# Side work spread inside the dense units: the delta rule's steps in a one-core hybrid flow step

## The chip, the core and the metric

The kernel runs on one core of a Trainium2 chip. The core has a matrix engine (TensorE, here PE, whose weight loads are listed apart as PEld), a vector engine (VectorE, DVE), a scalar engine (ScalarE, ACT), GpSimd (POOL) and SyncE (SP), which here issues most of the transfers (DMA). Each engine works off its own list of instructions, and semaphores order the lists against each other. The metric is the device time of one execution in microseconds (us); less is better.

## What is computed

The reference is one layer of a hybrid backbone, for 2048 tokens of one group (`x_sample`) and 128 of another (`x_prompt`), with D_MODEL = 1024 and branches of width 512. One wide projection feeds three token mixers, whose gated outputs are projected back and merged:

```python
proj = jnp.einsum('btd,de->bte', xn, w_in)
qkv, beta, dec, z_a, u_b, v_b, z_b, x_c, z_c, gates = jnp.split(proj, points, axis=-1)
qkv = short_conv(qkv, conv_w)
...
o, s_f, s_b = delta_bidir(q, k, v, g, beta, s0_f, s0_b)      # branch A: gated delta rule
o_a = (rmsnorm(o, o_norm_g) * jax.nn.silu(z_a)).reshape(B, T, W_BR)
o_b = chunk_sgu(u_b, v_b, sgu_norm_g, w_spatial, b_spatial) * jax.nn.silu(z_b)   # branch B
o_c = fourier_mix(x_c, grid) * jax.nn.silu(z_c)                                  # branch C
pb = jnp.einsum('btnw,nwd->btnd', br, w_branch)
merged = jnp.einsum('btnd,btnd->btd', jax.nn.sigmoid(gates), pb)
return jnp.einsum('btd,de->bte', merged, w_out), s_f, s_b
```

The delta rule goes over the tokens in chunks, forwards and backwards. Within a chunk a triangular system is solved, and from chunk to chunk a 128x128 state per head (four heads) is carried:

```python
def step(s, inp):
    u0_, w_, qk_, qg_, kd_, gl_ = inp
    u = u0_ - jnp.einsum('bhck,bhkv->bhcv', w_, s)
    o = jnp.einsum('bhck,bhkv->bhcv', qg_, s) + jnp.einsum('bhij,bhjv->bhiv', qk_, u)
    s = gl_[..., None, None] * s + jnp.einsum('bhck,bhcv->bhkv', kd_, u)
    return s, o
```

## The kernel before

**Dense work.** The normalised tokens lie in SBUF as two float16 halves, `xh` and `xl`. Every weight block of 128 columns is loaded by SP into one of two staging tiles `wst` (`read_w`, L185), squared and summed on ACT (L194), turned into a power-of-two scale (`scales`, L165 to L178: a cast and four small integer operations on DVE, L170 to L177, and one tiny matmul `wscb`), and split by ACT (L200) and DVE (L201) into the halves `whi` and `wlo`. A product is then three float16 matmuls for each 128 rows of the contraction. `gemm_T` makes outputs with channels on the partitions, for token blocks of 512 (the last has 128: `TBS`). `gemm_N` makes outputs with tokens on the partitions, 128 columns at a time in the V and Fourier stages, 512 at a time in the output stage. A dense *unit* is one such output block of eight 128-row products. All PE work goes through the helper `mm` (L159 and L160), so dense matmuls and many side matmuls carry L160; transposes have the lines of their callers.

**Stages, in order of the span.** Modulation and the first normalisation with the gate of branch A (to about 150 us); twelve q/k/v units with their convolution (to about 430); V of branch B with its spatial matmul (`wsT`, to about 560); U and the gate of branch B (from about 566 to 775); the Fourier branch (four channel groups, from about 775 to 1100: x columns by `gemm_N`, row transforms through the tiles `X20`, `X21`, then the gate); the branch projections and merges; the output projection.

**Side work.** The delta rule has little work per step and long chains of dependence, so its instructions are emitted in between. `delta()` is a Python generator that yields after each step: for each of 17 chunks `prep` (norms of q and k, transposes, the products k·k and q·k, stores), for each block of four chunks `base_inverse` (the inverse of 32x32 triangles on DVE: the tiles `XB` and `E`, loaded from DRAM by L713, started by the copy L716 after eight empty steps, then 31 rounds of L723 and L724), and then two scans of 17 chunks (`scan_dir`, `level`, `attend`). An earlier generator, `decays()`, makes the decay factors during the q/k/v stage.

**Pace.** The class `Pace` holds one generator. After a unit the kernel calls `pace.tick(us)` with the unit's length in us; the length is added up, and for every `quota` (1.2 us in `decays()`, 1.6 in `delta()`) one step is taken. A unit of 512 tokens counts 5.12 us, so three or four steps are emitted one behind another after it. `tick` also calls `weight_step()`, which takes one step of the weight pipeline: a load, or one of the three parts of a conversion.

**Who decides the order.** Python's order of emission is a priority. A scheduler orders each engine's list by these priorities and by its own model of when operands are ready; evictions of dense results stand under `tc.high_priority()`. The list that results is fixed, and on the chip each engine keeps to it. The PSUM banks of dense units come from a pool of three (`ps_mm`), those of side work from `ps_d`, and `ps_x` holds two more.

Of the kernel before, what the change touches and what calls it, by code (L numbers as in the profile page):

```python
# [20 lines left out]
P = 128  # L21
# [89 lines left out]
def hybrid_flow_kernel(ctx: ExitStack, tc: tile.TileContext, x_prompt, x_sample, state_delta, c, c_ctx, ln_g, w_ada,  # L111
# [44 lines left out]
    mhalf = sb(cp, [P, 1], "mhalf")  # L156
    G.memset(mhalf, -0.5)

    def mm(out, l, r, start=True, stop=True):  # L159
        PE.matmul(out, l, r, start=start, stop=stop)  # L160

    def rsqrt(out, ss, mul, w):
        G.tensor_scalar(out, ss, mul, EPS, ALU.mult, ALU.add)
# [60 lines left out]
    w_in_, w_ada_, b_ada_ = w_in[0], w_ada[0], b_ada[0]  # L224
    xs_, xp_ = x_sample[0], x_prompt[0]
# [84 lines left out]
    PE.transpose(pp.rearrange("p g k -> p (g k)"), prc, ident[:16, :16])  # L310
    sc = sb(cp, [P, 2, KT], "sc")
    A.activation(sc, pp, AF.Sigmoid)
    scT = sb(cp, [P, KT, 2], "scT")
# [5 lines left out]
    def columns():  # L319
        SY.dma_start(prm[0:8, :], ln_g.rearrange("o (k p) -> (o k) p", p=P))  # L320
        SY.dma_start(prm[8:44, :], conv_w[0].rearrange("t (k p) -> (t k) p", p=P))
        SY.dma_start(prm[44:48, :], sgu_norm_g.rearrange("o (k p) -> (o k) p", p=P))
        SY.dma_start(prm[48:49, :], o_norm_g)
        SY.dma_start(prm[49:65, :], b_ada[0, 0:2 * D].rearrange("(k p) -> k p", p=P))
        pp = bank(ps_x, [P, NPRM])
        PE.transpose(pp, prm, ident[:NPRM, :NPRM])
        V.tensor_copy(pc, pp)

    convw = lambda j, ct: pc[:, 8 + j * 12 + ct:8 + j * 12 + ct + 1]
# [26 lines left out]
    for blk in range(8):  # L356
        if blk == XB:
            load_x(*TBS[0])
            columns()
        ps = bank(ps_d, [2, 256])  # L360
        for k0 in range(0, KT, 4):
            st = sb(p0p, [P, 4, 256], "ast", bufs=8)
            last_ada = SY.dma_start(st, w_ada_[k0 * P:(k0 + 4) * P, blk * 256:(blk + 1) * 256].rearrange("(k p) c -> p k c", p=P))
            if k0 and blk in AD:
                acc = sb(p0p, [P, 2, 256], "aacc")
                ada_sum(acc, st, range(k0, k0 + 4))
                for g in range(2):
                    mm(ps, sel[:, g, :], acc[:, g, :], False, g == 1)
                continue
            for k in range(4):  # L370
                mm(ps, scT[:, k0 + k, :], st[:, k, :], k0 + k == 0, k0 + k == KT - 1)
        adr = sb(p0p, [2, 256], "adr")
        V.tensor_copy(adr, ps)
        for k in range(2):
            PE.transpose(pa[:, blk * 2 + k, :], adr[:, k * P:(k + 1) * P], ident[:2, :2])
    ms = sb(cp, [P, KT, 2], "ms")
    sh = sb(cp, [P, KT, 2], "sh")
    with tc.high_priority():
# [23 lines left out]
    for ti, (t0, tn) in enumerate(TBS):  # L402
# [13 lines left out]
        for k in range(KT):  # L416
            ps = bank(ps_d, [P, tn])
            for j in range(nt):
                PE.transpose(ps[:, j * P:(j + 1) * P], xt[:, j, k * P:(k + 1) * P], ident)
# [30 lines left out]
    def decays():  # L450
# [60 lines left out]
        gamR = dram("gamR", [2, NCH * H, P])  # L511
        for d in range(2):
            pt = bank(ps_d, [HN, P])
            PE.transpose(pt, flat(gam)[:, d * HN:(d + 1) * HN], ident)
# [111 lines left out]
    def prep(g, ci, t, nxt, held):  # L626
# [5 lines left out]
        def turned(part):  # L632
            ps = bank(ps_d, [P, WB])
            for h in range(H):
                PE.transpose(ps[:, hs(h)], cur[part][:, h, :], ident)  # L635
            return ps

        def norm(ps, i):
# [22 lines left out]
        T = sb(d2, [P, WB], "T")  # L661
        ps = bank(ps_d, [P, WB])
        for h in range(H):
            PE.transpose(ps[:, hs(h)], tok[:, 0, hs(h)], ident)
        A.copy(T, ps)
        A.dma_start(kTD[t], T)
        more(2, lambda: rows(2, nxt))
# [244 lines left out]
    def finish(t, o):  # L912
# [7 lines left out]
        V.tensor_tensor(h3(o), h3(o), bc(ss, P), ALU.mult)  # L920
        ps = bank(ps_out, [P, WB])
        for h in range(H):
            PE.transpose(ps[:, hs(h)], o[:, hs(h)], ident)  # L923
# [72 lines left out]
    vw = getw(4, 1)  # L996
    ps = bank(ps_x, [P, 4, P])
    for g in range(4):
        PE.transpose(ps[:, g, :], wsn[:, g, :], ident)
    V.tensor_copy(wsT, ps)  # L1000
    vinv = sb(ep, [P, 4], "vinv", bufs=1)
    for i in range(4):
# [383 lines left out]
```

## Time and profile before

| | |
|---|---|
| time, median of 3 runs | 2290.28 us (2284.63 to 2294.26) |
| time of the profiled execution | 2289.02 us |
| its span, first to last instruction | 2287.2 us |
| mean granted clock of PE | 0.993 |
| busy, share of the span | PE 97%, DVE 56%, ACT 34%, POOL 38% |
| matmul groups at L160 with 128x512 outputs, `xh·whi`, `xh·wlo`, `xl·whi` | 2080 each, 702.3, 703.9 and 704.3 us busy |
| ACT's wait for `wst` ahead of L194, in all | 174.2 us, 47 times, longest 10.7 |

A row of the timeline reads: start and duration in us, engine, line, operation, written tile <- read tiles, operands, the number of instructions merged into the row, and in brackets the idle time of the engine just before it with what ended it. A matmul's duration contains its way through the array: 128x512 matmuls that last 0.38 us each start 0.216 us apart. A float32 matmul is recorded as two passes. A row of the busy time by stages reads: stretch and its length, then busy time and number of instructions of PE, PEld, DVE, ACT and POOL, the granted clock of PE, the share of DMA, and GB/s. A row of the waits reads: total us, how often, the longest.

### The profile page before, as it was taken

The numbers are of one execution on the slowest core, as the hardware profiler recorded it, in microseconds if no ns is written. First come the engines' busy times: TensorE is split into PE (matmuls) and PEld (weight loads), VectorE is DVE, ScalarE is ACT, GpSimd is POOL, SyncE is SP. The second block draws the span as 40 slices with busy tenths as digits, with TensorE's granted clock in tenths as the row PEclk, the third lists the DMA queues.
The fourth block names the chain that finished last, engine by engine and source line by source line (L and its number), as shares of the span: only waits on it lengthen the run. The fifth ranks groups of instructions, "written<-read, shape, count | busy, mean of one in ns | idle before, by whom it ended". The sixth has DMA issues, their size and how long they took to land.

```text
span 2287.2 us, 43200 instructions
## 1 busy us (share of the span) xinstructions
PE 2229.7 (97%) x17076; PEld 1365.7 (60%) x17076; DVE 1283.9 (56%) x3001; ACT 769.0 (34%) x1485; POOL 861.3 (38%) x1090
## 2 busy tenths in 40 slices
PE   7999999999999999999999999999999999999998
PEld 3564444798555787788566666566665444444443
DVE  5637744496857666455655446756665443333454
ACT  3544633322333332332422223433322332222232
POOL 1421332253546430553433324355653121122643
PEclk9999999999999999999999999999999999999999
DMA  8416722376777543343634344655554444332542
GB/s 275 144 52 205 245 103 81 115 226 162 232 216 227 161 139 69 117 134 108 206 122 133 122 133 140 205 161 171 171 158 149 148 131 130 111 114 95 186 150 101
DMA packets 320628, 345.92 MB, mean 151 GB/s; under 512 B 52641, under 2 KB 242058, under 8 KB 318378
## 3 DMA queue, kind: packets, MB, share of 16 engines
q1 hardware_dynamic: 303114, 278.53, 40.4%
q0 software_dynamic: 12416, 51.27, 6.1%
q10 hardware_dynamic: 4896, 13.37, 1.5%
q8 instruction: 134, 2.20, 0.4%
q14 instruction: 68, 0.56, 0.1%
HBM read 219.94 MB, written 123.17 MB: 150 GB/s over the span
## 4 chain that ended last, share of the span: by engine, by line
PE 58%; DVE 7%; DMA 5%; ACT 1%; issue 1%; POOL 1%; SPq 1%; DVEq 0%; POOLq 0%; ACTq 0%
PE b L160 57%; DMA wst<-in_w_in_dram 1%; DMA st<-br 1%; DVE XB L723 1%; DVE E L724 1%; DVE big L1180 1%; DVE wlo L201 0%; DVE n L677 0%; DMA mt<-mrg 0%; PE b L635 0%; PE b L923 0%; DMA mrow<-mrg 0%; ACT big L1179 0%; DMA e<-ei 0%; SPq L734 0%
## 5 line engine op out<-in xcount | busy, mean ns | idle before, releaser
L160 PE MATMUL b<-xh,whi 128*128 128x512 f16 (+1 forms) x2080 | 702.3, 348 | 6.8 <-ACT whi L200 2.2
L160 PE MATMUL b<-xh,wlo 128*128 128x512 f16 (+1 forms) x2080 | 703.9, 348 | 0.7 <-DVE wlo L201 0.7
L160 PE MATMUL b<-xl,whi 128*128 128x512 f16 (+1 forms) x2080 | 704.3, 348 | 0.1
L160 PEld LDWEIGHTS <-whi 128*128 128x128 f16 x4224 | 392.6, 98 | 380.2 <-issue 10.2
L160 PEld LDWEIGHTS <-wlo 128*128 128x128 f16 x2112 | 206.9, 98 | 193.0 <-issue 2.8
L160 PE MATMUL b<-big,bhi 128*128 128x512 f16 (+1 forms) x960 | 250.2, 347 | 1.6 <-ACT big L1179 0.8
L1219 POOL TENSOR_TENSOR mrow<-mrow,sg 128x512 f32<-128x512 f32 (+1 forms) x80 | 91.6, 1146 | 301.5 <-DVE sg L1218 170.8
L160 PE MATMUL b<-whi,xh 128*128 128x128 f16 x1088 | 188.5, 221 | 1.8 <-DVE sg L972 1.8
L160 PE MATMUL b<-wlo,xh 128*128 128x128 f16 x1088 | 188.4, 221 | 0.0
L160 PE MATMUL b<-whi,xl 128*128 128x128 f16 x1088 | 188.2, 221 | 0.0
L160 PEld LDWEIGHTS <-xh 128*128 128x128 f16 x2312 | 177.8, 99 | 2.7 <-issue 1.9
L160 PE MATMUL b<-big,blo 128*128 128x512 f16 (+1 forms) x480 | 163.0, 347 | 0.0
L863 POOL TENSOR_SCALAR skn<-skn,ed 128x128 f32<-128x128 f32 x136 | 81.5, 615 | 197.4 <-DMA skn<-kv 175.4
L160 PEld LDWEIGHTS <-bhi 128*128 128x128 f16 x960 | 89.4, 98 | 85.9 <-ACT big L1179 1.0
L1209 ACT ACTIVATE sg<-b,winv 128x512 f32<-128x512 f32 (+1 forms) x120 | 74.3, 620 | 197.2 <-PE b L160 196.6
L581 POOL TENSOR_TENSOR cy<-cy,raw 128x545 f32<-128x545 f32 (+1 forms) x48 | 66.3, 1406 | 194.1 <-ACT raw L580 194.1
L1218 DVE SCALAR_TENSOR_TENSOR sg<-b,binv,sg 128x512 f32<-128x512 f32 (+1 forms) x80 | 53.5, 669 | 150.4 <-PE b L160 146.7
L194 ACT ACTIVATE wlo<-wst 128x1024 f16<-128x1024 f32 x60 | 63.3, 1056 | 179.2 <-DMA wst<-in_w_in_dram 174.2
L160 PEld LDWEIGHTS <-xl 128*128 128x128 f16 x1224 | 114.3, 98 | 0.4
L759 POOL TENSOR_TENSOR R<-ec,cst 128x512 f16<-128x512 f16 x68 | 73.1, 1095 | 79.3 <-PE b L160 71.9
L201 DVE SCALAR_TENSOR_TENSOR wlo<-wst,wsc,whi 128x1024 f16<-128x1024 f32 x60 | 80.7, 1346 | 35.1 <-ACT whi L200 34.9
L759 POOL TENSOR_TENSOR T<-ec,cst 128x512 f16<-128x512 f16 x68 | 75.3, 1127 | 59.6 <-PE b L160 48.5
(390 smaller groups left out, 3821.6 us busy)
## 6 DMA issues: line engine op xcount, KB each, us to landing
wst<-in_w_in_dram SPq DMA_DIRECT2D x60, 512.0 KB
qkv<-cy POOLq DMA_DIRECT2D x12, 1089.0 KB, 5.2
st<-br SPq DMA_DIRECT2D x48, 256.0 KB
mrow<-mrg SPq DMA_DIRECT2D x18, 512.0 KB
mrow<-mrg SPq DMA_DIRECT2D x16, 576.0 KB
mrg<-mrow POOLq DMA_DIRECT2D x16, 576.0 KB, 3.7
dc<-dec SPq DMA_DIRECT2D x17, 512.0 KB
kq<-qkv SPq DMA_DIRECT2D x34, 256.0 KB
```

The source lines that it names most:

```text
L160: PE.matmul(out, l, r, start=start, stop=stop)
L194: A.activation(w.lo, st, AF.Square, accum_out=ss)
L201: V.scalar_tensor_tensor(w.lo, st, s, w.hi, ALU.mult, ALU.subtract)
L581: G.tensor_tensor(y[:, c0:c1], y[:, c0:c1], raw[:, 1 + c0:1 + c1], ALU.mult)
L723: V.tensor_tensor(t3, X3[:, 0:k, k:k + 1].to_broadcast([P, k, n_]), E3[:, k:k + 1, k:32].to_broadcast([P, k, n_]), ALU.mult)
L724: V.tensor_tensor(E3[:, 0:k, k:32], E3[:, 0:k, k:32], t3, ALU.subtract)
L759: G.tensor_tensor(dst[:, l].rearrange("p h a b c -> p h (a b) c"), wide(ec[:, :, which ^ d, l, :]), bm, ALU.mult)
L863: G.tensor_scalar(kn_[:, hs(h)], kn_[:, hs(h)], ed[:, d, t, h:h + 1], None, ALU.mult)
L1180: V.scalar_tensor_tensor(o16[:, 1, g, t0:t0 + tn], st, s, o16[:, 0, g, t0:t0 + tn], ALU.mult, ALU.subtract)
L1209: A.activation(sg, ps, AF.Sigmoid, scale=gw.inv)
L1218: V.scalar_tensor_tensor(sg, ps, binv[:, 1:2], sg, ALU.mult, ALU.mult)
L1219: G.tensor_tensor(mr, mr, sg, ALU.add)
```

## The change

A wrapper `placed` is put around every matmul and every transpose (`transpose` replaces the nine direct calls). While a step of the side generator runs, `turn["side"]` is true, and each PE instruction of that step gets an ordering edge behind the last PE instruction emitted outside of a step. The edge is of a kind that needs no semaphore, since both are on PE; it keeps the scheduler from putting a side matmul ahead of the dense ones that were emitted before it.

`Pace` gets a second entrance, `inside(us)`, that is called within the units: in `gemm_T` after the second, fourth and sixth of eight 128-row products, with 1.28 us for 512 tokens (not for the 128-token block), and in `gemm_N` with 1.3 us after a 128-column product. What was counted inside is taken off the next `tick`, so the number of steps per unit stays the same in the long run. `weight_step()` is still taken only in `tick`. `inside` does nothing when no generator is running, which is so ahead of the q/k/v stage and after the delta rule's end.

```diff
+    turn = {"side": False, "dense": None}
+
+    def placed(i):
+
+        if not turn["side"]:
+            turn["dense"] = i.ins.name
+        elif turn["dense"] is not None:
+            tc.add_manual_dep(i.ins, turn["dense"], mybir.DependencyInfo(mybir.DependencyClass.NoSync, mybir.DependencyReason.DATA), reason="side work")
+
+    def transpose(out, a, i):
+        placed(PE.transpose(out, a, i))
+
     def mm(out, l, r, start=True, stop=True):
-        PE.matmul(out, l, r, start=start, stop=stop)
+        placed(PE.matmul(out, l, r, start=start, stop=stop))
...
             mm(ps, w.lo[:, k, c0:c0 + P], rh[:, k, :], False, stop and k == nkt - 1)
+            if k % 2 and k < nkt - 1 and rh.shape[-1] > P:
+                pace.inside(rh.shape[-1] / 400)
...
             mm(ps, ll[:, k, :], w.hi[:, k, c0:c0 + n], False, k == nkt - 1)
+        if n == P:
+            pace.inside(1.3)
...
     class Pace:
         def __init__(self):
-            self.gen, self.acc, self.quota = None, 0.0, 1.0
+            self.gen, self.acc, self.quota, self.inner = None, 0.0, 1.0, 0.0
...
         def tick(self, us):
+
             weight_step()
+            us, self.inner = max(0.0, us - self.inner), 0.0
+            self.count(us)
+
+        def inside(self, us):
+            if self.gen is not None:
+                self.inner += us
+                self.count(us)
+
+        def count(self, us):
             self.acc += us
             while self.gen is not None and self.acc >= self.quota:
                 self.acc -= self.quota
+                turn["side"] = True
                 if next(self.gen, 0) == 0:
                     self.gen = None
+                turn["side"] = False
...
-                PE.transpose(ps[:, hs(h)], cur[part][:, h, :], ident)
+                transpose(ps[:, hs(h)], cur[part][:, h, :], ident)
```

The last pair stands for all the transposes, which change in the same way.

More of the change, by code (lines that the diff above doesn't have):

```diff
@@ L309, in hybrid_flow_kernel @@
     pp = bank(ps_x, [P, 2, KT])
-    PE.transpose(pp.rearrange("p g k -> p (g k)"), prc, ident[:16, :16])
+    transpose(pp.rearrange("p g k -> p (g k)"), prc, ident[:16, :16])
     sc = sb(cp, [P, 2, KT], "sc")
@@ L325, in columns @@
         pp = bank(ps_x, [P, NPRM])
-        PE.transpose(pp, prm, ident[:NPRM, :NPRM])
+        transpose(pp, prm, ident[:NPRM, :NPRM])
         V.tensor_copy(pc, pp)
@@ L374, in hybrid_flow_kernel @@
         for k in range(2):
-            PE.transpose(pa[:, blk * 2 + k, :], adr[:, k * P:(k + 1) * P], ident[:2, :2])
+            transpose(pa[:, blk * 2 + k, :], adr[:, k * P:(k + 1) * P], ident[:2, :2])
     ms = sb(cp, [P, KT, 2], "ms")
@@ L418, in hybrid_flow_kernel @@
             for j in range(nt):
-                PE.transpose(ps[:, j * P:(j + 1) * P], xt[:, j, k * P:(k + 1) * P], ident)
+                transpose(ps[:, j * P:(j + 1) * P], xt[:, j, k * P:(k + 1) * P], ident)
             t = sb(p0p, [P, tn], "xm", bufs=3)
@@ L513, in decays @@
             pt = bank(ps_d, [HN, P])
-            PE.transpose(pt, flat(gam)[:, d * HN:(d + 1) * HN], ident)
+            transpose(pt, flat(gam)[:, d * HN:(d + 1) * HN], ident)
             gr = sb(a1p, [HN, P], "gr", bufs=1)
@@ L663, in prep @@
         for h in range(H):
-            PE.transpose(ps[:, hs(h)], tok[:, 0, hs(h)], ident)
+            transpose(ps[:, hs(h)], tok[:, 0, hs(h)], ident)
         A.copy(T, ps)
@@ L922, in finish @@
         for h in range(H):
-            PE.transpose(ps[:, hs(h)], o[:, hs(h)], ident)
+            transpose(ps[:, hs(h)], o[:, hs(h)], ident)
         SY.dma_start(h3(of), szD[:, :, t * P:(t + 1) * P].rearrange("h p t -> p h t"))
@@ L998, in hybrid_flow_kernel @@
     for g in range(4):
-        PE.transpose(ps[:, g, :], wsn[:, g, :], ident)
+        transpose(ps[:, g, :], wsn[:, g, :], ident)
     V.tensor_copy(wsT, ps)
```

## The prediction

> **What bounds the kernel now.** I read the page's busy times first, then the chain of waits, then the busy time by stages, then the waits of TensorE (PE) inside the stretch that the change can reach.
>
> ```profile
> span 2287.2 us, 43200 instructions
> ...
> PE 2229.7 (97%) x17076; PEld 1365.7 (60%) x17076; DVE 1283.9 (56%) x3001; ACT 769.0 (34%) x1485; POOL 861.3 (38%) x1090
> ...
> PE 58%; DVE 7%; DMA 5%; ACT 1%; issue 1%; POOL 1%; SPq 1%; DVEq 0%; POOLq 0%; ACTq 0%
> ```
>
> PE is busy for 97% of the span and its own work is over half of the chain that ended last. The change issues the same matmuls, so it can only alter the 57.5 us in which PE is idle (2287.2 - 2229.7) and the time for which PE runs at a lower clock. The order of the two built programs says where: on all five engines the instructions stand identically up to about 150 us and after about 1243 us of the old time, when the delta rule has ended. Between these, PE's order differs in 4624 of its 15883 places, VectorE's (DVE) in 1090 of 3003, ScalarE's (ACT) in 393 of 1300.
>
> ```profile
> 150.00:430.00 280.00, 278.59 (x1836) 142.42 (x1834) 154.92 (x201) 127.32 (x193) 72.27 (x95) 1.00 0.42 142
> 430.00:560.00 130.00, 127.11 (x1907) 123.49 (x1905) 97.57 (x253) 38.26 (x78) 61.33 (x116) 1.00 0.60 185
> 560.00:800.00 240.00, 229.42 (x1573) 140.22 (x1571) 171.14 (x435) 81.04 (x152) 119.51 (x194) 0.99 0.72 209
> 800.00:930.00 130.00, 127.76 (x1382) 105.03 (x1380) 78.67 (x204) 45.35 (x95) 38.81 (x62) 1.00 0.44 114
> 930.00:1243.00 313.00, 303.02 (x2931) 221.89 (x2929) 175.31 (x464) 103.44 (x255) 126.59 (x145) 0.98 0.42 133
> ```
>
> The second column is PE's busy time and the seventh its granted clock. PE's idle time here is 1.41 + 2.89 + 10.58 + 2.24 + 9.98 = 27.1 us. That, with a few us of lower clock, is all that the change can win, while what it can lose has no such bound.
>
> **What the change moves.** It adds no instruction on any engine, and the ordering constraint is between instructions of one engine, so it costs nothing by itself. What moves is the order. A step of the delta rule was emitted in bursts after a dense unit; now one is emitted after every 1.28 us of dense work. A weight's own steps (its Square and conversion on ACT, its load on SP) are still taken only after a unit, so they fall behind delta steps that they preceded. The dense matmuls keep their order; groups of side matmuls shift by some 5 us of dense work either way. I therefore went through every operand that PE waits for and asked what now stands ahead of its producer on DVE and ACT, each of which runs its own list in order. Four places carry the sum.
>
> **Removed: Squares that wait for a load, ahead of small casts.**
>
> ```profile
> 939.62 1.06 ACT L194 ACTIVATE wlo<-wst 128x1024 f16<-128x1024 f32 x1 [6.80 <-DMA wst<-in_w_in_dram]
> 941.09 0.27 ACT L796 ACTIVATE R<-b 32x128 f16<-32x128 f32 x1
> 941.70 0.27 ACT L801 ACTIVATE T<-b 32x128 f16<-32x128 f32 x1 [0.35 <-DVE R L797]
> 942.34 0.82 PE L160 MATMUL b<-T,sn 128*128 128x64 f16 x12 [5.23 <-DVE T L802]
> 942.30:946.40 4.10, 4.06 (x45) 4.06 (x46) 1.32 (x3) 0.83 (x2) 2.25 (x2) 0.50 0.22 64
> ```
>
> ACT sat 6.80 us before a weight's Square (L194), with two 0.27 us casts of the scan behind it, and PE waited 5.23 us for what comes of them. Then PE ran for 4.10 us at a granted clock of 0.50, which costs half of it, 2.05 us. In the new order both casts stand ahead of that Square. PE also reaches their matmuls some 2 us of dense work earlier, so I leave 1 us of wait: -(5.23 + 2.05 - 1.0) = -6.3 us (bounds -7.3 and, if the casts' input is late as well, -4).
>
> ```profile
> 1105.73 0.63 ACT L194 ACTIVATE blo<-wst 128x512 f16<-128x512 f32 x1 [6.05 <-DMA wst<-in_w_branch_dram]
> 1107.86 1.16 PE L160 MATMUL b<-S,sq__1602_13572 128*128 128x128 f32 x8 [0.99 <-DVE wsc L173]
> 1109.26 0.52 PE L160 MATMUL b<-T,sn 128*128 128x64 f16 x12 [0.25 <-DVE T L802]
> 1110.63 0.61 PE L160 MATMUL b<-big,bhi 128*128 128x512 f16 x1 [0.85 <-ACT big L1179]
> 1110.60:1114.00 3.40, 3.37 (x9) 1.26 (x10) 3.37 (x8) 1.99 (x6) 2.33 (x2) 0.55 0.87 261
> ```
>
> The same at 1106 us: a Square behind a 6.05 us wait holds two casts. The three PE waits shown (0.99 + 0.25 + 0.85 = 2.1 us) and 3.40 us at a clock of 0.55 (1.5 us) go, -3.6 us, if nothing takes their place; the cast of `big` (L1179) is reordered too, so the other end is 0. A wait of 1.4 us at 184 us is covered by the new order as well:
>
> ```profile
> PE b L160 <- DVE ed L507: 1.4, 1, 1.4
> ```
>
> Gains: 6.3 + 3.6 + 1.4 = 11.3 us.
>
> **Added: the copy of XB ahead of a weight's scale chain, at 566 us.**
>
> ```profile
> 564.41 0.15 DVE L176 TENSOR_SCALAR wsc<-wsc 128x1 int32<-128x1 int32 x1
> 564.90 2.18 ACT L200 ACTIVATE whi<-wst,wsc 128x1024 f16<-128x1024 f32 x2
> 566.10 0.39 PE L160 MATMUL b<-xh,whi 128*128 128x512 f16 x1 [2.22 <-ACT whi L200]
> 569.39 1.05 DVE L716 COPY XB<-XB 64x1024 f32<-64x1024 f32 x1 [4.45 <-DMA XB<-nd]
> 571.75 0.20 DVE L723 TENSOR_TENSOR XB<-XB,E 128x31 f32<-128x31 f32 x1
> ```
>
> Here the V phase goes over to the U phase. DVE makes the scale of U's first weight at 564.4 (L176), ACT the weight itself (two in 2.18 us, so 1.09 each), and PE starts on it at 566.1. DVE's copy L716 comes later and waits 4.45 us for its load. In the new order the copy stands ahead of L175 to L177. I see no reason for its load to land sooner by more than 1 us: the loads are issued when the block's last store is done. So the copy ends at 569.39 + 1.05 = 570.4, two short instructions of the inverse and three of the scale follow (0.5 us by their rows' spacing), the weight is there at 570.9 + 1.1 = 572.0, and PE starts 6.0 us later than before. Moreover PE has then 12 f32 side matmuls fewer behind it (transposes of the next chunk and a product, now placed later). Eight such matmuls, in two passes each, take 1.95 us with the tail of the last in the row at 825 quoted below, so 12 take 2.7 us. The old 0.7 us wait for this unit's other half goes. That is 6.0 + 2.7 - 0.7 = +8.0 us, and PE has been idle for over 10 us, so a stretch of half clock follows as it did at 942: +1.8 us, the mean of the 2.05 and 1.5 above. Bounds: +4 if the load lands 4 us earlier, +12 if the copy also waits for loads that are now issued between its own.
>
> **Added: the same copy at 480, 673 and 770 us.**
>
> ```profile
> 475.09 1.11 DVE L1010 SCALAR_TENSOR_TENSOR vs<-b,pc,bsp 128x128 f32<-128x128 f32 x4
> 478.74 0.68 DVE L641 TENSOR_REDUCE ss<-sq 128x4 f32<-128x512 f32 x1
> 480.38 1.07 DVE L716 COPY XB<-XB 64x1024 f32<-64x1024 f32 x1 [0.96 <-DMA XB<-nd]
> 482.38 1.16 PE L160 MATMUL b<-wsT,sg 128*128 128x128 f32 x8 [1.05 <-DVE sg L1033]
> ...
> 673.52 1.07 DVE L716 COPY XB<-XB 64x1024 f32<-64x1024 f32 x1 [4.11 <-DMA XB<-nd]
> 673.55 0.60 PE L664 MATMUL b<-cst,tok 128*128 128x128 f32 x4
> ...
> 762.99 0.69 DVE L653 TENSOR_TENSOR tok<-b,ss 128x512 f32<-128x512 f32 x1 [2.85 <-POOL ss L643]
> 767.39 0.60 PE L664 MATMUL b<-cst,tok 128*128 128x128 f32 x4
> 769.86 1.05 DVE L716 COPY XB<-XB 64x1024 f32<-64x1024 f32 x1 [5.41 <-DMA kq<-qkv]
> ```
>
> At 770 the product `tok` (L653) was done 6 us ahead of the copy, and at 673 it was as well; now it stands behind it, a reduction (0.6 us from start to start) and one or two instructions of the inverse (0.25 each). At 673: 673.52 + 1.07 + 0.35 for a small gate product + 0.5 + 0.6 + 0.68 = 676.7, and PE came to `tok`'s transposes at 673.6: +3.1 us. At 770: 769.86 + 1.05 + 0.6 + 0.25 + 0.69 = 772.4; PE came at 767.4 and has four dense matmuls more ahead of them in the new order (0.22 each by the spacing of such rows), so it is there at 768.3: +4.1 us. At 480 a product, a reduction (0.6 each) and four evictions (1.1 together) come between the copy and the scaling L1033 that ended PE's wait at 482.4: +2.3 us. Together +9.5 us. Low end 0, if the loads land before their neighbours are due; high end +13, if two of the waits bring a stretch of lower clock. The fifth copy, at 871 us, has nothing of weight behind it.
>
> **Added: X20 behind a Square, at 825 us.**
>
> ```profile
> 821.68 0.37 ACT L1116 COPY X<-b 128x252 f32<-128x252 f32 x1 [0.49 <-DVE X L1115]
> 825.67 1.95 PE L160 MATMUL b<-cf,X 128*128 128x128 f32 x16
> 828.61 1.06 ACT L194 ACTIVATE wlo<-wst 128x1024 f16<-128x1024 f32 x1 [6.56 <-DMA wst<-in_w_in_dram]
> 829.66 0.61 ACT L681 ACTIVATE n<-n 128x512 f16<-128x512 f32 x1
> ```
>
> The mirrored half of a Fourier tile (L1116) came before the Square; now the Square and a cast stand ahead of it: 828.61 + 1.06 + 0.55 + 0.37 = 830.6, and 0.4 for DVE's half is 831.0. PE has one transform matmul and five dense ones to do from 825.67 and is ready for the rest at 827.0: +4.0 us, and +1.7 for the clock. Low end 0 (if the load lands before 824), high end +6.
>
> For the rest (a second half of a weight at 251 us, the scan from 890 to 1100) I take +1 us, between -3 and +5.
>
> **The sum.** 8.0 + 1.8 + 9.5 + 5.7 + 1.0 - 11.3 = +14.7 us. Waits in one chain overlap (a PE that comes late finds the next operand ready), so I take off the clock stretch at 825, of which I am least sure, 1.7: +13. The profiled execution took 2289.0 us, 1.3 below the median of the three runs, so 2290.3 + 13 = 2303 us, 0.6% slower.
>
> The rows do not say how much idling brings the half clock: 5.23 us did, and so did two shorter waits together:
>
> ```profile
> 776.92 0.22 PE L160 MATMUL b<-whi,xh 128*128 128x128 f16 x1 [1.81 <-DVE sg L972]
> 779.25 1.11 PE L635 MATMUL b<-cst,kq 128*128 128x128 f32 x4 [1.95 <-DVE n L677]
> 776.00:784.00 8.00, 5.13 (x53) 4.89 (x53) 7.97 (x24) 4.01 (x9) 6.40 (x12) 0.79 0.36 106
> ```
>
> So any of the new waits of 2 to 4 us may bring it, or not, as the 2.22 us at 566 did not: between one stretch (+13) and five (8.0 + 9.5 + 4.0 + 1.0 + 5 x 1.8 - 11.3 = +20); I keep the lower, because of the overlaps. [...]
>
> **Rivals.** (1) Faster: the producers are out sooner as their steps are spread, so the loads of XB and of the weights that I held fixed are issued sooner and land before the work behind them is due; the new waits shrink to their low ends (4 + 0 + 0 + 0) while the gains stay, and half of the other PE waits go. 4 - 11.3 - 0.5 x (27.1 - 5.2 - 2.1 - 1.4) = -16.5 us: 2274 us. For it: DMA is no bound (share 0.42 to 0.72). Against it: XB's loads hang on stores of the same chunk, which do not move. It decides if the copy at 566 runs before 565. Chance 0.13. (2) Nothing that can be measured: the new waits come half as long and cancel the gains, 2290 us +/- 8. For it: the dense order is untouched and 90% of PE's work has its operands long before. Chance 0.27. (3) Clearly slower: PE cannot pass a late side matmul, each late step delays the next chunk's loads, and the ends add up: 12 + 13 + 6 + 5 - 4 = +32, less the overlaps of about 6: 2316 us. For it: DVE is 71% busy from 560 to 800 (171.14 of 240), so that what falls behind there stays behind. Chance 0.18. The forecast, 2295 to 2310, has 0.42.
>
> **Range and chances.** All low ends together are 4 - 7.3 - 3.6 - 1.4 - 3 = -11 us, the high ones +32; I leave out the outer tenth on each side: 2281 to 2318. A run of this kernel can be told from no change at about 0.5%, 11.4 us: faster is below 2278.8, slower above 2301.7. Faster has 0.13; slower has rival 3 and 0.29 of the forecast's 0.42, together 0.47; the rest, 0.40, is the same.
>
> **What would show it.** After the change ACT's wait ahead of L206 (the old L194) no longer has the scan's casts behind it, and PE has no 5 us wait at the T,sn matmuls. PE waits some 10 us ahead of the U phase's first weight (at 561 to 572 us) with a granted clock well under 1 behind it, 3 to 4 us at `tok`'s transposes near 673 and 770, and 4 us at the X20 transforms near 827. The forecast is wrong if the first weight of U is ready before 568 or the stretch from 1243 us on, 1044.2 us long, changes by more than its own spread.

## The result, and the profile after

The changed kernel takes 2299.85 us (median of 4 runs, 2297.29 to 2300.76), the kernel before 2289.2 us in the 4 runs beside it (2284.63 to 2294.26). The ratio is 1.0037, with a 95% interval of 1.0023 to 1.0052: 0.4% slower. When both were run again in the last comparison, the ratio was 1.0055 [1.0040, 1.0070]. The profiled execution of the changed kernel took 2299.02 us.

The page of the changed kernel, the same three lines as before:

```profile
span 2297.2 us, 43199 instructions
...
PE 2232.9 (97%) x17076; PEld 1367.9 (60%) x17076; DVE 1275.3 (56%) x3001; ACT 770.0 (34%) x1485; POOL 862.6 (38%) x1090
...
PE 76%; DMA 8%; DVE 8%; ACT 2%; issue 2%; SPq 2%; POOL 2%; DVEq 0%; POOLq 0%; ACTq 0%
```

The span is 10.0 us longer. PE is idle for 2297.2 - 2232.9 = 64.3 us where it was 57.5, so 6.8 us of the loss are waits; the 3.2 us by which PE is busy longer with the same matmuls are work at a lower clock (0.991 on the mean, 0.993 before). Waits for loads have a larger share of the chain that ended last (8% for 5%). Busy time by stages, in the same columns as before (stretch, length, PE, PEld, DVE, ACT, POOL, clock, DMA share, GB/s), with a row for part of the time in which both kernels have the same order:

```profile
150.00:430.00 280.00, 278.89 (x1842) 142.52 (x1839) 155.39 (x199) 127.52 (x194) 75.16 (x98) 1.00 0.42 142
430.00:560.00 130.00, 124.61 (x1898) 123.52 (x1896) 97.87 (x253) 38.52 (x76) 59.63 (x114) 0.99 0.60 182
560.00:800.00 240.00, 225.80 (x1463) 133.12 (x1463) 165.47 (x419) 79.41 (x150) 112.73 (x189) 0.99 0.71 208
800.00:930.00 130.00, 123.05 (x1224) 99.95 (x1223) 79.53 (x213) 41.03 (x84) 28.21 (x51) 0.97 0.39 99
930.00:1243.00 313.00, 303.12 (x3097) 228.37 (x3095) 168.35 (x455) 106.64 (x261) 135.80 (x155) 0.99 0.43 137
1243.00:2000.00 757.00, 756.45 (x5482) 441.30 (x5481) 409.91 (x1056) 233.71 (x488) 291.76 (x320) 1.00 0.48 150
```

PE's idle time in the first five rows is 1.11 + 5.39 + 14.20 + 6.95 + 9.88 = 37.5 us, against 27.1 before. These windows no longer hold the same work in both kernels, so I also followed PE from one dense matmul to the next. The dense matmuls keep their order, so the n-th is the same work in both. Lost time is the sum, over all PE instructions in between, of what each start-to-start distance has beyond the usual one for its form; it holds waits and half clock alike. I call this account the ledger. By old times:

| from one dense matmul to another (us, before) | term of the prediction | predicted | measured |
|---|---|---|---|
| 173 to 352 | the wait at 184 | -1.4 | -1.6 |
| 448 to 484 | copy of XB at 480 | +2.3 | +3.6 |
| 558 to 617 | V to U: the copy ahead of the scale | +9.8 | +4.6, then -2.5 |
| 617 to 729 | copy of XB at 673 | +3.1 | +2.8 |
| 764 to 783 | copy of XB at 770 | +4.1 | -1.8 |
| 820 to 843 | X20 behind a Square | +5.7 | +6.6 |
| 894 to 916 | none | | +8.1 |
| 936 to 1000 | Square ahead of casts, 942 | -6.3 | -6.5 |
| 1100 to 1180 | the same, 1107 | -3.6 | -4.4, then +2.0 |
| rest of 173 to 1257 | rest, less 1.7 for overlap | -0.7 | +1.4 |
| sum, 173 to 1257 | | +13.0 | +12.3 |

Ahead of 173 us it is 1.2 us before the first dense matmul and 1.4 us behind it; from 1257 us on it is -4.9 us. That makes 12.3 + 2.6 - 4.9 = 10.0, the difference of the spans.

**V to U.** The timeline of the changed kernel (L744 is the old L716, L188 the old L176, L212 the old L200, L172 the old L160; transposes now have the line of their helper, L169), and the clock behind the wait:

```profile
568.29 0.16 PE L172 MATMUL b<-wscb,ones 128*128 128x1 bf16 x1 [0.98 <-DVE vs L1038]
571.40 1.03 DVE L744 COPY XB<-XB 64x1024 f32<-64x1024 f32 x1 [3.10 <-DMA XB<-nd]
572.72 0.14 DVE L188 TENSOR_SCALAR wsc<-wsc 128x1 int32<-128x1 int32 x1
572.90 2.19 ACT L212 ACTIVATE whi<-wst,wsc 128x1024 f16<-128x1024 f32 x2 [11.97 <-DVE wsc L188]
574.10 0.61 PE L172 MATMUL b<-xh,whi 128*128 128x512 f16 x1 [5.64 <-ACT whi L212]
```

```profile
574.10:576.90 2.80, 2.80 (x7) 1.01 (x8) 2.80 (x5) 0.98 (x1) 0.00 (x0) 0.50 0.81 264
```

The copy stands ahead of the scale, as predicted. It waits 3.10 us for its load, ACT waits 11.97 us for the scale, PE 5.64 us for the weight. The half clock, of which the row shows 2.80 us, lasts until 577.25 us.

**X20.** In the timeline ACT's copy of the mirrored half (L1144, the old L1116) now stands behind the Square (L206, the old L194), whose load ends a wait of 7.89 us; PE waits 4.81 us for what follows:

```profile
828.32 0.38 ACT L1142 COPY X<-b 128x260 f32<-128x260 f32 x1 [1.53 <-PE b L172]
837.16 1.06 ACT L206 ACTIVATE wlo<-wst 128x1024 f16<-128x1024 f32 x1 [7.89 <-DMA wst<-in_w_in_dram]
838.74 0.35 ACT L1144 COPY X<-b 128x252 f32<-128x252 f32 x1
840.03 3.29 PE L172 MATMUL b<-cf,X 128*128 128x128 f32 x14 [4.81 <-DVE X L1145]
```

```profile
840.00:843.50 3.50, 3.47 (x16) 3.50 (x17) 1.29 (x3) 0.51 (x2) 0.00 (x0) 0.51 0.20 75
```

**What the sum did not have.** At 935 us PE waits 4.47 us for a PSUM bank of the Fourier stage that DVE's `yT` (L1160) has to read out. `yT` needs ACT's copy `us` (L1155), and ACT is held by the cast `ec` (L778) of the first scan step, which waits 9.92 us for the load of `e`. Before, `us` stood ahead of `ec`. The timeline, and the clock behind it:

```profile
933.15 0.42 ACT L778 ACTIVATE ec<-e 128x256 f16<-128x256 f32 x1 [9.92 <-DMA e<-ei]
933.47 0.35 ACT L1155 COPY us<-b 128x256 f32<-128x256 f32 x1
934.89 0.59 DVE L1160 TENSOR_TENSOR yT<-b,us 128x256 f32<-128x256 f32 x1
935.54 0.23 PE L172 MATMUL b<-whi,xh 128*128 128x128 f16 x1 [4.47 <-DVE yT L1160]
```

```profile
935.50:939.00 3.50, 3.46 (x34) 3.46 (x35) 0.59 (x2) 0.42 (x1) 3.50 (x4) 0.52 0.57 168
```

4.47 us and half of 3.5 us make the 6.2 us that the ledger has between the old 914 and 916 us. The other 1.9 us of the 8.1 in the table are not the cast's: they are lost near 917 us, where half clock follows two short waits (the rows are in the last section). The kernel before has the same two waits at 902 us, of 1.28 and 0.54 us, with the full clock behind them.

**The gains.** The two casts of the scan (L824 and L829, the old L796 and L801) come before the Square that held them. The wait ahead of that Square is 0.69 us, and PE has no wait over 0.25 us there. At the second place 1.33 us are left of 6.05:

```profile
953.98 0.27 ACT L824 ACTIVATE R<-b 32x128 f16<-32x128 f32 x1 [1.29 <-DVE R L820]
954.69 0.27 ACT L829 ACTIVATE T<-b 32x128 f16<-32x128 f32 x1
957.20 1.06 ACT L206 ACTIVATE wlo<-wst 128x1024 f16<-128x1024 f32 x1 [0.69 <-DMA wst<-in_w_in_dram]
...
1126.01 0.63 ACT L206 ACTIVATE blo<-wst 128x512 f16<-128x512 f32 x1 [1.33 <-DMA wst<-in_w_branch_dram]
1130.21 0.51 PE L172 MATMUL b<-T,sn 128*128 128x64 f16 x12
```

### The profile page after: what moved, and what is told of

Its sections match the earlier page's. It is cut to its first block, busy times and chain, and to the rows that moved or that the text cites. A ratio compares the mean times of both kernels' runs of the same rounds, so it can differ in the third digit from the quotient of the medians.

```text
span 2297.2 us, 43199 instructions
## 1 busy us (share of the span) xinstructions
PE 2232.9 (97%) x17076; PEld 1367.9 (60%) x17076; DVE 1275.3 (56%) x3001; ACT 770.0 (34%) x1485; POOL 862.6 (38%) x1090
## 4 chain that ended last, share of the span: by engine, by line
PE 76%; DMA 8%; DVE 8%; ACT 2%; issue 2%; SPq 2%; POOL 2%; DVEq 0%; POOLq 0%; ACTq 0%
PE b L172 74%; DMA wst<-in_w_in_dram 2%; PE b L169 2%; DVE E L752 1%; DVE XB L751 1%; DMA st<-br 1%; SPq L391 1%; POOL nd L707 1%; SPq L762 1%; DMA xt<-in_x_sample_dram 1%; DVE n L705 1%; DMA qk<-n 1%; DMA kq<-qkv 0%; ACT wlo L206 0%; DMA of<-o 0%
## 5 line engine op out<-in xcount | busy, mean ns | idle before, releaser
L172 PE MATMUL b<-xh,whi 128*128 128x512 f16 (+1 forms) x2080 | 702.2, 348 | 6.8 <-ACT whi L212 5.6
L172 PE MATMUL b<-xl,whi 128*128 128x512 f16 (+1 forms) x2080 | 704.0, 348 | 0.5 <-POOL xl L451 0.4
L172 PE MATMUL b<-xh,wlo 128*128 128x512 f16 (+1 forms) x2080 | 703.1, 348 | 0.1
L172 PEld LDWEIGHTS <-whi 128*128 128x128 f16 x4224 | 392.0, 98 | 377.7 <-ACT whi L212 7.1
L172 PEld LDWEIGHTS <-wlo 128*128 128x128 f16 x2112 | 206.4, 98 | 192.2 <-issue 2.7
L172 PE MATMUL b<-big,bhi 128*128 128x512 f16 (+1 forms) x960 | 250.3, 347 | 2.5 <-ACT big L1207 1.7
L172 PE MATMUL b<-whi,xh 128*128 128x128 f16 x1088 | 188.7, 221 | 4.5 <-DVE yT L1160 4.5
L172 PE MATMUL b<-wlo,xh 128*128 128x128 f16 x1088 | 189.0, 221 | 0.0
L172 PE MATMUL b<-whi,xl 128*128 128x128 f16 x1088 | 189.0, 221 | 0.0
L172 PEld LDWEIGHTS <-xh 128*128 128x128 f16 x2312 | 177.5, 98 | 5.7 <-DVE yT L1160 4.6
L172 PE MATMUL b<-big,blo 128*128 128x512 f16 (+1 forms) x480 | 163.1, 348 | 0.0
L172 PEld LDWEIGHTS <-bhi 128*128 128x128 f16 x960 | 89.4, 98 | 84.0
L206 ACT ACTIVATE wlo<-wst 128x1024 f16<-128x1024 f32 x60 | 63.3, 1055 | 179.7 <-DMA wst<-in_w_in_dram 174.7
L172 PEld LDWEIGHTS <-xl 128*128 128x128 f16 x1224 | 114.0, 98 | 0.3
L182 DVE CAST wscb<-wss 128x1 bf16<-128x1 f32 x93 | 14.4, 155 | 151.3 <-ACT wlo L206 140.4
```

Of the source, the lines that this page charges most:

```text
L172: placed(PE.matmul(out, l, r, start=start, stop=stop))
L206: A.activation(w.lo, st, AF.Square, accum_out=ss)
```

## The experiments

The theory that they test: spreading the steps is worth a few us by itself; the loss comes from single instructions that wait for a load and now stand ahead of an eviction or cast that PE needs, on ACT or DVE, which keep to their lists (at 933 us above, `us` starts 0.32 us after `ec` and its wait of 9.92 us). The rivals: the ordering edges make the loss; or a repaired wait is covered and comes back at the next late load. The ratios below are to the kernel before on the same chip, with 95% intervals; its medians there were 2293.18, 2293.34 and 2293.48 us. The changed kernel itself ran beside it only twice, in the first comparison (1.0037) and in the last (1.0055); other versions are set against these two.

**The two parts of the change, each alone.** The first experiment drops the edges, the second the calls inside the units:

```diff
-        elif turn["dense"] is not None:
-            tc.add_manual_dep(i.ins, turn["dense"], mybir.DependencyInfo(mybir.DependencyClass.NoSync, mybir.DependencyReason.DATA), reason="side work")
```

> The steps are emitted inside the units, but the ordering edges between PE instructions are left out. Theory (what stands ahead of what on VectorE and ScalarE makes the waits): the copy of XB is still ahead of the scales at about 570 us and the Square still ahead of X20's second half at about 837 us, but the first cast of the scan (ec, L778) is back behind the eviction us, so only the 4.5 us wait at 935 us and its 1.6 us of half clock go: about 2294 us. Rival (the edges hold side matmuls back on PE, and that is the loss): the whole +10 us goes, about 2289 us, with the waits at 574 and 840 us gone.

Measured: 2297.45 us, 1.0022 [1.0011, 1.0033]. The theory's 2294 us is 1.0021 of the 2289.2 us that it was reckoned from, and the rival's 1.000 lies outside the interval. In its trace the wait for `yT` is gone, while that at V to U (6.3 us) and that at X20 (4.4 us) are still there, and the gains at 942 and 1107 remain.

```diff
-            if k % 2 and k < nkt - 1 and rh.shape[-1] > P:
-                pace.inside(rh.shape[-1] / 400)
...
-        if n == P:
-            pace.inside(1.3)
```

> The ordering edges alone, with steps emitted after the units as before. Theory: in this order only ec (L778) moves ahead of the eviction us; the copy of XB, X20 and the Squares stand as before, so the 5 us wait at 942 us stays, a wait of 4 to 5 us appears near 920 us with half clock behind it, and the time is about 6 us above before, 2295 us. Rival (edges cost nothing by themselves): 2289 us. Rival (edges are the whole loss): 2299 us or more.

Measured: 2297.57 us, 1.0015 [1.0005, 1.0024]. Its timeline:

```profile
925.14 0.42 ACT L774 ACTIVATE ec<-e 128x256 f16<-128x256 f32 x1 [9.55 <-DMA sn<-n]
927.53 0.29 PE L172 MATMUL b<-whi,xh 128*128 128x128 f16 x1 [3.86 <-DVE yT L1156]
...
949.56 1.06 ACT L206 ACTIVATE wlo<-wst 128x1024 f16<-128x1024 f32 x1 [1.28 <-DMA wst<-in_w_in_dram]
```

The edges alone bring the wait behind `ec`: with them the scheduler puts the cast ahead of `us`. Two things were not expected: the 5 us wait at 942 did not stay, as the Square there waits only 1.28 us with both casts still behind it; and the ledger has +5.3 us from 558 to 617 us, against -7.2 us from 936 to 1000. The two halves, 0.22% and 0.15%, make the 0.37% of the whole, but each is uncertain by 0.1%, and the repeat of the whole has 0.55%.

**The copy of XB put back.** `kept` remembers the newest and the last-but-one instruction of a name, and the copy gets an edge behind the last-but-one of `winv` (the last step of a weight's scale) and of `tok`:

```diff
...
+    def behind(i, names):
+        for n in names:
+            if n in last:
+                tc.add_manual_dep(i.ins, last[n], mybir.DependencyInfo(mybir.DependencyClass.NoSync, mybir.DependencyReason.DATA), reason="side work")
...
-        V.tensor_mul(w.inv, inv, isx)
+        kept("winv", V.tensor_mul(w.inv, inv, isx))
...
-        V.tensor_copy(b3(X[64:P, :]), tmp[64:P, :].rearrange("p (i j) -> p j i", j=32))
+        behind(V.tensor_copy(b3(X[64:P, :]), tmp[64:P, :].rearrange("p (i j) -> p j i", j=32)), ("winv", "tok"))
```

> The changed kernel with the copy of XB ordered on VectorE behind the last but one weight scale and tok. Theory: the wait of PE at 574 us falls from 5.8 to at most 2.4 us and its half clock goes, the ones at 683 and 780 us fall below 0.5: -5 to -7 us, about 2294 us. Rival (the load of XB sets the pace, so the wait turns up elsewhere, in the inverse's users): no change, 2300 us.

Measured: 2302.72 us, 1.0038 [1.0024, 1.0052]. The theory's 2294 us (1.0021) missed, and against the changed kernel's 1.0037 there is no gain, as the rival has it. The wait ahead of U's first weight fell to 1.50 us and the waits behind the copies near 680 and 780 are gone, but a new one stands some 50 us later, with half clock behind it:

```profile
566.21 0.39 PE L184 MATMUL b<-xh,whi 128*128 128x512 f16 x1 [1.50 <-ACT whi L224]
...
621.65 0.90 PE L181 MATMUL b<-cst,qr 128*128 128x128 f32 x4 [2.96 <-issue]
```

Against the changed kernel the ledger has -4.0 us at V to U, +8.5 us in the stretch behind it, and -3.1 us from 617 to 729. The variant with `winv` alone:

```diff
-        behind(V.tensor_copy(b3(X[64:P, :]), tmp[64:P, :].rearrange("p (i j) -> p j i", j=32)), ("winv", "tok"))
+        behind(V.tensor_copy(b3(X[64:P, :]), tmp[64:P, :].rearrange("p (i j) -> p j i", j=32)), ("winv",))
```

> The changed kernel with the copy of XB ordered behind the last but one weight scale alone, so that at 570 us it stands right behind the scales of U's first two weights, and not behind tok some 15 us later. Theory (the 574 us wait is a matter of order, and f1 gave it back at 622 us because it moved the copy too far): the wait at 574 us falls to about 1.6 us, no new wait over 1 us appears near 622 us, those at 683 and 780 us stay: 4 to 6 us less than the changed kernel, ratio to before about 1.0015. Rival (any later copy is paid for later in the chunk's chain): ratio as the changed kernel's, 1.0037.

Measured: 2308.9 us, 1.0071 [1.0054, 1.0088]: the theory missed, and the rival's 1.0037 is exceeded as well. The wait at 574 is gone (-5.7 us against the changed kernel), but PE comes to the second weight of U too early:

```profile
582.01 1.06 ACT L218 ACTIVATE wlo<-wst 128x1024 f16<-128x1024 f32 x1 [6.50 <-DMA wst<-in_w_in_dram]
583.40 0.16 PE L184 MATMUL b<-wscb,ones 128*128 128x1 bf16 x1 [2.48 <-DVE wscb L194]
```

In the changed kernel the same Square starts 2 us later, at 583.99 us, and PE, held up at 574, does not have to wait for it. So the load of the second weight sets the pace here, and the wait at 574 for the most part only stood in front of it. Between 617 and 729 us the ledger has 5.4 us more than the changed kernel, in waits for `sg` and ahead of `qr` near 648 us and the half clock behind them.

**`ec` put back behind `us`**, with the same helper, which here remembers the newest `us`, for the first step of a scan:

```diff
-        A.activation(ec[:, :, :, 0, :], e32, AF.Copy, scale=FS)
+        behind(A.activation(ec[:, :, :, 0, :], e32, AF.Copy, scale=FS), ("us",) if t == 16 else ())
```

> The changed kernel with the cast ec of each scan's first chunk ordered on ScalarE behind the last eviction us. Theory: the 4.5 us wait at 935 us (yT, L1160) and 1.6 us of half clock go: about 2294 us. Rival (the scan then starts later and its end is the bound, or the load's wait moves to the next instruction): 2300 us.

Measured: 2303.71 us, 1.0050 [1.0035, 1.0065]: no gain is shown, as it lies between the changed kernel's two ratios. The wait at 935 is gone (-6.2 us in the ledger), 3.7 us come back at the scan's matmuls between 945 and 960 us, and the stretch ahead of 930 us, in which the order is that of the changed kernel, took 4 to 6 us longer in this trace. So the place of the loss is confirmed; that the whole loss there can be won back by this edit is not shown.

**X20's two copies together.** The second copy on ACT is emitted directly behind the first, so that no Square comes between:

```diff
                 A.copy(X2[:, :, 0, 0:65], ps[:, :, 0:65])
-                V.tensor_copy(X2[:, :, 0, 127:64:-1], ps[:, :, 1:64])
                 A.copy(X2[:, :, 1, 1:64], ps[:, :, 65:P])
+                V.tensor_copy(X2[:, :, 0, 127:64:-1], ps[:, :, 1:64])
```

> The changed kernel with the two ScalarE copies of a Fourier tile X2 emitted one behind the other, so that the Square that waits for its load no longer stands between them. Theory: PE's wait at 840 us (5.0 us) and 1.5 us of half clock go: 6 to 7 us less, ratio to before about 1.001. Rival (the wait for the load is met by the next user on ScalarE, and PE waits there): as the changed kernel, 1.0037.

Measured: 2294.98 us, 1.0006 [0.9998, 1.0015]. Its timeline:

```profile
834.27 0.38 ACT L1142 COPY X<-b 128x260 f32<-128x260 f32 x1 [1.53 <-PE b L172]
834.54 0.37 ACT L1143 COPY X<-b 128x252 f32<-128x252 f32 x1
839.71 1.95 PE L172 MATMUL b<-cf,X 128*128 128x128 f32 x16
842.37 1.06 ACT L206 ACTIVATE wlo<-wst 128x1024 f16<-128x1024 f32 x1 [6.92 <-DMA wst<-in_w_in_dram]
```

The Square still waits 6.92 us, but both copies stand ahead of it and PE's 4.81 us wait is gone; the ledger has -6.7 us at this place, and the interval lies below both of the changed kernel's. The same edit in the kernel before, as the control:

> The kernel before with the same reordering of X2's halves, as a control: there the two copies already stand together, so the time stays, ratio 1.000 +/- 0.001. If X2's order is worth something by itself, it is under 0.998.

Measured: 2294.61 us, 1.0001 [0.9991, 1.0011]. The edit does nothing where the copies stood ahead of the Square anyway.

**Without edges, with X20 repaired.** The changed kernel with the first experiment's lines removed and X20's two copies together, at first also with the XB copy behind `winv` (the helper and the edits of that experiment), then without:

> Steps inside the units without the PE edges (+5 us against before), with both orders above mended (X2's halves together, XB's copy behind the scales). Theory: the waits at 570 and 832 us go, the gains at 942 and 1107 us stay: 5 - 5 - 7 = -7 us against before, ratio 0.997. Rival (mended waits come back elsewhere): 1.001 to 1.003.

Measured: 2288.27 us, 0.9980 [0.9969, 0.9990]: the theory's 0.997 is within the interval, the rival's 1.001 is not.

> Steps inside the units without the PE edges, with X2's halves together, and XB's copy left where the change puts it. Theory (the wait at 570 us is mostly given back by loads that come late anyway): e1's 1.0022 less the 7.3 us at 832 us, about 0.999, 2 us above h2. Rival (the copy ahead of the scales costs its full 6.5 us): 1.001.

Measured: 2286.61 us, 0.9971 [0.9960, 0.9981], 6.9 us faster than the kernel before. That is better than the theory's 0.999, and the rival's 1.001 is out. The version with XB's copy behind the scales is not faster than this one. The wait of 7.2 us at V to U is still in its trace; the ledger has +5.1 us there and -2.5 us in the stretch behind it.

**Which units.** The same version with the steps inside `gemm_N` alone:

```diff
-            if k % 2 and k < nkt - 1 and rh.shape[-1] > P:
-                pace.inside(rh.shape[-1] / 400)
```

> As h1, but the steps are emitted inside the token-major units only (V and the Fourier x columns, gemm_N), not in gemm_T. In its order the scan's first casts stand ahead of the Square, so the 5.2 us wait at 942 us and 2 us of half clock go; XB's copies at 673 and 770 us stand as before; the Squares of the branch weights near 1107 us still stand between the casts. At 566 us the copy of XB stands ahead of the last evictions of V: theory, +2 to +5 us there. In all 2 to 5 us less than before, ratio 0.998 to 0.999. Rival (the gain at 942 us needs the steps inside both kinds of units): 1.000 or more.

Measured: 2298.07 us, 1.0021 [1.0013, 1.0030]: the rival. Its timeline at V to U:

```profile
569.17 1.03 DVE L740 COPY XB<-XB 64x1024 f32<-64x1024 f32 x1 [8.67 <-DMA XB<-nd]
571.41 0.16 PE L170 MATMUL b<-wscb,ones 128*128 128x1 bf16 x1 [5.00 <-DVE vs L1034]
```

The copy got ahead of V's last evictions (L1034) too and waits 8.67 us there. The ledger has +8.0 us, with 2.4 us given back behind it. At the scan's start the gain of 6.8 us is there, but 5.6 us are lost just ahead of it, the longest wait (2.5 us) for the cast `Q`; so little of the gain is left, as the rival has it. With the steps inside `gemm_T` alone:

```diff
-        if n == P:
-            pace.inside(1.3)
```

> As h1, but inside gemm_T only. In its order the Square still stands ahead of the scan's first casts, so the 942 us wait stays; the casts near 1107 us stand behind the Squares no longer (-4 us); XB's copy is ahead of the scales at 570 us (+2.5) and of tok at 673 and 770 us (+2). About as before, ratio 0.999 to 1.001, and 3 to 6 us above j1.

Measured: 2285.9 us, 0.9968 [0.9956, 0.9979]: better than expected, and with the version that has the steps in both kinds of units (0.9971) the best of all. Its wait at the scan's start is 3.0 us where it was 5.2, and at the old 1107 the ledger has some 5 us less.

**The changed kernel once more**, for the spread of a trace:

> The changed kernel itself again, beside the others on one chip: ratio to before 1.003 to 1.005; with it f1 (1.0038) and f2 (1.005) are to be read as no gain. If it comes out at 1.005 or more, f1 is a gain of some us after all.

Measured: 2306.45 us, 1.0055 [1.0040, 1.0070], 13.0 us above the kernel before. By the expectation the first XB experiment, at 1.0038, is then a gain of some us after all. The intervals overlap, and its lost time from 173 to 1257 us is 2.7 us above the changed kernel's first trace and 2.4 below this one, so whether it gains stays open. In this trace the ledger has 69.4 us of lost time from 173 to 1257 us where the first had 64.3, and 26.9 us behind 1257 us where the first had 20.6, with the same program. The two timelines that follow are of the kernel before and of this one:

```profile
1480.59 0.25 PE L160 MATMUL b<-R,Q 128*64 128x64 f16 x2 [2.98 <-ACT Q L810]
```

```profile
1500.94 0.25 PE L172 MATMUL b<-R,Q 128*64 128x64 f16 x2 [4.21 <-ACT Q L838]
```

This wait is absent from the first trace of the changed kernel and from that with `gemm_T` alone, and is there, with 2.4 to 4.4 us of lost time, in the twelve other traces, whatever the kernel. So the -4.9 us behind 1257 us can't be put down to the change, and a difference of about 5 us between two ledgers says little unless a row shows the wait that makes it.

## Why the prediction was right

The forecast was 2303 us, 0.6% slower; 0.4% was measured, and 0.55% in the repeat. Within the change's reach the sum was +13 us; the ledger has +12.3, and +17.5 in the repeat's trace. The terms for X20 and for 942 held to within a microsecond in both traces. Those for V to U and for the XB copies were too large, by 7.7 and 4.9 us (8.4 and 0.3 in the repeat), and one of 8.1 us was missing. The direction and the kind of wait were right; that the sum came out as it did is in part luck. By the prediction's own line of 0.5% the first result counts as the same, which had 0.40, and the repeat as slower, which had 0.47.

- **Squares ahead of casts (held).** Predicted -6.3 us at 942, measured -6.5. At 1107 -4.4 us stand against -3.6, but 2.0 us of it come back at later waits for `big` and `R`, as the other end of the bounds allowed. The gain at 184 came too; 1.4 us were lost just ahead of it, at 175.
- **X20 (held).** Predicted a 4.0 us wait and 1.7 us of half clock, measured 4.81 us and 3.5 us at 0.51. The 1.7 us that I took off for overlap should have stayed. The experiment with the copies together shows the cause, and its control that the cause lies in the change.
- **V to U (right in mechanism, mis-sized).** The term was +9.8 us, the net loss 2.1. The copy and its load behaved as predicted, 2 us later instead of earlier, and U's first weight was ready at 574.1 us, past the 572.0 of the forecast. But by then PE was itself 6.1 us later, so that it idled for 0.98 and 5.64 us instead of over 10. Of the 4.6 us lost, 2.5 came back, since the waits behind it that the kernel before has, for `wlo`, `wscb`, `qr` and `sg` between 573 and 616 us, are gone when PE comes later. I had priced the new wait and not asked which old ones it stands in for. With the wait taken away (the two XB experiments) waits for `wscb`, `tok` and `qr` stand there again, the longest of 2.48 and 2.96 us.
- **The XB copies at 480, 673 and 770 (mis-sized).** Predicted +9.5 us, measured 4.6 over these stretches (9.2 in the repeat, so the size is not settled), and less of it through the copy. At 480 it did not wait at all; PE's loss there is two waits for loads of `kq` and one ahead of `qr`. Near 680 and 778 the copy stands ahead of the products as predicted, and PE waits 0.73 and 1.67 us for the rounds of the inverse behind it, not 3.1 and 4.1 us for `tok` (1.99 and 3.10 us in the repeat). At 780 the old 1.81 us wait for `sg` is gone in exchange. Rows of the changed kernel's timeline:

```profile
481.77 1.05 DVE L744 COPY XB<-XB 64x1024 f32<-64x1024 f32 x1
483.65 0.63 PE L169 MATMUL b<-cst,qr 128*128 128x128 f32 x4 [2.21 <-issue]
...
679.03 1.06 DVE L744 COPY XB<-XB 64x1024 f32<-64x1024 f32 x1 [4.55 <-DMA XB<-nd]
682.53 0.63 PE L169 MATMUL b<-cst,tok 128*128 128x128 f32 x4 [0.73 <-DVE E L752]
...
777.41 1.04 DVE L744 COPY XB<-XB 64x1024 f32<-64x1024 f32 x1 [7.33 <-DMA XB<-nd]
780.02 0.63 PE L169 MATMUL b<-cst,tok 128*128 128x128 f32 x4 [1.67 <-DVE E L752]
```

- **`ec` ahead of `us` (missing).** The rest was put at +1 us, between -3 and +5; this one place cost 6.2 (8.0 in the repeat), and the half clock near 917 us another 1.9, which the repeat does not have. It is the same pattern as the others, an instruction with a load to wait for, placed ahead of an eviction. I had looked for it at the producers of PE's operands and not at the instructions that free its PSUM banks.
- **The clock (under-counted).** I kept to the low end of one new stretch of half clock, so that all clock terms of the sum make -1.8 us and its waits +14.8. Five new stretches came, at 458, 570, 840, 919 and 936 us, and the three old ones, at 779, 940 and 1110, went. Half of PE's busy time within them is 8.2 us after and 5.2 before, so +3.0. The waits came as 37.5 - 27.1 = +10.4. The waits were overrated by 4.4 us and the clock underrated by 4.8, and the two cancel: that is the luck in the sum. In the repeat's trace the waits are +13.9 us and the half clock +3.9.
- **The stretch behind 1243 us.** I gave it as the end of the delta rule. That was wrong: the scans run on until 1747.7 us, and only the order of the instructions is the same from 1243 us on. The prediction needs no more than the order. By the repeat its 4.9 us are within its own spread.
- **The range.** By its own rule its low end is 2283 us and not 2281: -11.3 us and a tenth of 43 make -7. Nothing hangs on it.

Of the rivals, the third (all ends add up, 2316 us) did not come. The second (2290 us +/- 8, nothing that can be measured) did not either: 10.7 and 13.0 us were measured, and both intervals leave out no change. Its reason, new waits that come shorter, held at V to U. The first (faster) failed at the point that was to decide it: the copy ran at 571.4, not before 565. That the edges cost nothing by themselves is shown only in that they add no instruction on PE (17076 in both kernels): through the order that the scheduler made with them they brought the wait behind `ec`, 3.86 us with the edges alone.

Three things stay open. The three kernels without edges and with X20 repaired that beat the kernel before do so by 5 to 8 us, but their ledgers show only 1 to 3 us of it between 173 and 1257 us; that is no contradiction, as the one trace of the kernel before is of an execution of 2289.02 us, 4 us below its medians beside these kernels, and the stretch behind has too large a spread. So which waits make the gain is not shown. Why the edges alone took the wait at 942 away was not tried. Nor was the edge behind `winv` and `tok` on the best version.

## What to carry to other kernels

When side work is emitted in finer pieces, go through each engine's list for instructions that wait for a load, and see what now stands behind them: operands of PE as well as evictions that free its banks. Here such places (X20, `ec`, V to U and XB) cost more than the finer spread won, and moving one copy by one place, with the edges left out, turned +0.4% into -0.3%. Price a new wait against the old waits behind it: where the next load is late anyway, part of it is already paid for, as at V to U, where 2.5 of the 4.6 us lost came back.

## What the runs showed of the hardware

Half clock came after two short waits as well. Around 917 us PE waits 1.10 and 0.97 us, with 0.49 us of work between:

```profile
916.96 0.49 PE L172 MATMUL b<-cf,X 128*128 128x128 f32 x2 [1.10 <-DVE X L1143]
918.42 0.89 PE L172 MATMUL b<-cf,Y 128*128 128x128 f32 x3 [0.97 <-ACT yT L1180]
```

In all 14 traces the granted clock changes only on a fixed grid of 3.41 us, and each of the 71 stretches of half clock between 60 and 2270 us lasts 3.41, 6.83 or (once) 10.24 us. So a stretch of 3.41 us costs at most half of that, 1.7 us. The busy time of the changed kernel, by stretches of its grid:

```profile
454.37:457.79 3.42, 1.00 (x11) 0.65 (x8) 2.89 (x11) 1.31 (x3) 0.98 (x3) 1.00 1.11 358
457.79:461.20 3.41, 2.92 (x23) 2.89 (x24) 0.99 (x4) 1.63 (x2) 0.68 (x3) 0.50 1.12 347
...
481.68:485.09 3.41, 1.44 (x22) 1.46 (x23) 3.28 (x7) 1.79 (x4) 2.11 (x5) 1.00 1.06 357
485.09:488.50 3.41, 3.41 (x52) 3.41 (x50) 3.31 (x12) 0.00 (x0) 2.55 (x4) 1.00 0.92 239
...
915.17:918.59 3.42, 1.35 (x10) 0.97 (x9) 3.27 (x9) 1.75 (x4) 0.00 (x0) 1.00 0.00 0
918.59:922.00 3.41, 3.41 (x17) 3.41 (x18) 1.47 (x4) 0.75 (x2) 0.00 (x0) 0.50 0.72 106
```

In the stretch up to 457.79 us PE idles for 2.42 us, in that up to 918.59 for 2.07; both times the next stretch has half clock. The single wait of 2.21 us that ends at 483.65 leaves 1.97 us of idle time in its stretch, and the next has the full clock. By the profile's busy times, between 80 and 2270 us of the 14 traces, all 60 stretches at full clock with more than 2.04 us of idle time are followed by half clock, and no stretch with less than 1.66 us is; of the 40 in between 11 are. So in these traces the half clock went with the idle time within a stretch of the grid, in two waits near 917 us (2.07 us) as in one at 840 us (3.36 of its 4.81 us in one stretch); of the 2.21 us 0.24 lie in the stretch before.
